# First branch's merge products issued directly behind the gate projections, in the attention's PSUM banks and in buffers of the normed input

## The chip, the core and the metric

One core of a Trainium2 chip runs the whole kernel as one program. The metric is the device time of one execution in microseconds (us), as a median over runs. Engines by their names in the profile: PE is the TensorE matmul unit, PEld its weight loads, DVE the VectorE, ACT the ScalarE, POOL the GpSimd, SP the SyncE, which issues most DMAs. Each engine works through its own instructions strictly in the order of its list, and waits for the other engines by semaphores.

## The reference

One layer over 1024 tokens of width 1024. Cut to what matters here:

```python
h = rmsnorm(x, g_pre_mix)
proj = h @ w_in                 # S5 input, conv inputs, q, k, v, forget logits, 3 x 1024 gate logits
y_a = s5_mixer(...)             # (1024 tokens, 512)
y_b = short_conv_mixer(...)     # (1024, 512)
y_c = forgetting_attention(...) # (1024, 512), 8 heads x 64, causal
gates = sigmoid(gate_logits + b_gate)          # three gates of 1024 channels
merged = (gates[0] * (y_a @ wa) + gates[1] * (y_b @ wb) + gates[2] * (y_c @ wc))
mix = merged @ w_out
x = x + rmsnorm(mix, g_post_mix)
x = x + rmsnorm(squared_relu(rmsnorm(x, g_pre_mlp) @ w_ff1) @ w_ff2, g_post_mlp)
```

The three branches a, b, c are numbered 0, 1, 2 in the kernel. The three products with `wa`, `wb`, `wc`, weighted by the gates and summed, are the "merge".

## The kernel before

**Number format.** Every matmul operand is kept as a pair of float32r tiles, a high part (H) and the rest (L), made by `split` (lines 72 to 77): ACT copies the operand into H, DVE subtracts H from the operand into L. `mm3` issues three matmuls per pair (H·H, H·L, L·H). A product over 512 input channels, 128 output channels and 512 tokens is thus 4 x 3 = 12 matmuls into one PSUM bank.

**Order of the work.** The input projections come first, fed by the generator `proj_stream` from the list `todo`; the attention follows, and takes the rest of the projections as filler between its own steps: the gate projections `g0` to `g22`, the last of them held back in `reserve`. Each gate tile goes through `proj` (tile `p_g`, tag `pj`, 2 PSUM banks), `gate_cons` applies a tanh on ACT into an SBUF tile of pool `gp` (tag `gt`, 2 buffers), and a DMA stores it to DRAM (`gt_s`). Within the attention, `scores` makes a score bank `ps` (tag `s`, 2 buffers), DVE takes its maximum, ACT the exponential into `P`, DVE scales it; `trans` transposes `P` on PE (`pt`) and splits it into `PT`; `av_` multiplies with V (`av`) and ACT (`lo`) and DVE (`yc`) take the result out. Head group 3's `yc` is stored to DRAM last (line 1061).

**After the attention** the pools of the attention are closed. Branch outputs of the first token half (`th` = 0) were stored to DRAM and are read back by `y_load` (tile `yr`, 1 MB in four DMAs, into the tag `raw` of pool `ws`, 2 buffers, shared with every raw weight tile), and split by `y_split` into `yH` and `yL` in pool `ext` (tag `e8`, 6 buffers). Branch 0's output lies time-major, so its four pieces are read with strides. Then 24 merge products per token half follow: `merge_item(th, dp, b)` does two of them, for the output tiles 2·dp and 2·dp + 1 of branch b, in the order b = 0, 1, 2 for each dp. Each needs its weight (`r_wb` loaded, split to `wb_0H` and `wb_0L`, 3 buffers each), its y pair, and a gate tile read back from DRAM (`gl`, 4 buffers). The product stands in a PSUM tile `pb` of pool `mp` (tag `m`, 8 banks). For b = 0 DVE writes gate x product to the accumulator `ma` (pool `mg`); for b = 1, 2 DVE writes it in place of the gate and POOL adds it to `ma`. After b = 2, `ma` is split into the tiles `m` (pool `big`, tag `t8`, 8 buffers: the same ones that held the normed input `hT`). `run_items` loads weights up to two items ahead and splits one item ahead. The second half's `yr` tiles, the four output projections `wo` and so on follow.

**What decides where an instruction stands.** The program is written in the order above, but except inside the blocks marked `manual_schedule` the engines' lists are made by a scheduler at build time, which may pull later work up into earlier work. A buffer of a rotating tag is handed on when its last reader is done; the waiting is done by the first writer of the new tile, in its engine's queue.

## Time and profile before

| what | value |
|---|---|
| median of 3 runs | 1704.85 us (1703.64 to 1709.92) |
| profiled execution, its own time | 1708.72 us |
| its span, first to last instruction | 1707.0 us |
| PE busy | 1622.3 us, 95% of the span |
| DVE, ACT, POOL busy | 1029.8, 693.2, 499.0 us |
| DMA moved | 261.73 MB, 153 GB/s over the span |
| mean granted TensorE clock | 0.980 |

The page of the profile gives busy times and groups; the timeline lists instructions in time with, in square brackets, how long the engine sat idle before one and who ended that; the view of waits sums these; the windows view gives, per stretch, each engine's busy time with its instruction count, the granted clock, the DMA share and GB/s. Names are tile names without their numbers, output on the left of the arrow. SPq and ACTq rows are DMA issues. A matmul's row shows its latency; successive rows overlap, so the pace is read from the differences of starts.

### The profile page before, as it was taken

To read this page: it belongs to the slowest core of one execution; us is meant where nothing else is said; L and a number is where in the kernel's file an instruction comes from. 1 tells how busy PE (TensorE), PEld (TensorE's weight loads), DVE (VectorE), ACT (ScalarE), POOL (GpSimd) and SP (SyncE) were. 2 spreads that over 40 slices of the span, in tenths; PEclk is the share of its full clock that TensorE was granted. 3 is DMA by queue.
4 is the path that set the end of the run, shared out by engine and by line. 5 is a ranking of instruction groups with operands and counts; after the bars stand their busy time and mean duration, and the time that the engine had idled before them with its cause. 6 is when DMAs were issued, how large, how long until landed. Compare 5 with 4: busy or idle time off the path is not lost.

```text
span 1707.0 us, 21044 instructions
## 1 busy us (share of the span) xinstructions
PE 1622.3 (95%) x7815; PEld 1335.7 (78%) x7815; DVE 1029.8 (60%) x1548; ACT 693.2 (41%) x1042; POOL 499.0 (29%) x603
## 2 busy tenths in 40 slices
PE   7999999999999999997899989699999999999998
PEld 6778778879888787876677768578778878888886
DVE  4768655433264564655564674778888765545565
ACT  4312112231354554555343234554454454443442
POOL 1085643100422303120232552344434300101143
PEclk9999999999999999999899989899999999999999
DMA  5412322330744526331872562356654499755521
GB/s 161 121 41 77 83 86 82 112 93 10 239 152 167 185 75 228 100 142 39 266 250 93 184 223 87 105 161 192 197 189 142 156 334 383 259 198 187 184 99 50
DMA packets 186034, 261.73 MB, mean 153 GB/s; under 512 B 24752, under 2 KB 108764, under 8 KB 183884
## 3 DMA queue, kind: packets, MB, share of 16 engines
q1 hardware_dynamic: 170380, 228.93, 41.9%
q10 hardware_dynamic: 15552, 31.46, 4.9%
q8 instruction: 61, 1.00, 0.2%
q14 instruction: 41, 0.34, 0.1%
HBM read 183.54 MB, written 75.63 MB: 152 GB/s over the span
## 4 chain that ended last, share of the span: by engine, by line
PE 68%; DVE 8%; DMA 4%; POOL 4%; ACT 3%; issue 3%; SPq 1%; DVEq 0%; ACTq 0%; POOLq 0%
PE p_g L122 14%; PE P L122 12%; PE p_q L122 4%; PE pb L122 3%; PE pv L122 3%; PE P4f L122 3%; PE P7f L122 3%; PE P6f L122 3%; PE P5f L122 3%; PE P2f L122 3%; PE P3f L122 3%; PE P1f L122 2%; PE ps L122 2%; PE av L122 2%; PE pt L126 2%
## 5 line engine op out<-in xcount | busy, mean ns | idle before, releaser
L65 DVE TENSOR_TENSOR st<-x,st 128x1024 fp32r<-128x1024 f32 x70 | 86.7, 1251 | 77.5 <-ACT st L73 74.5
L122 PE MATMUL p_g<-hT,w_g_1H 128*128 128x512 f32 x384 | 126.8, 408 | 4.7 <-ACT g L831 3.5
L122 PE MATMUL p_g<-hT,w_g_0H 128*128 128x512 f32 x384 | 126.5, 406 | 2.8 <-DVE ac L65 2.8
L73 ACT ACTIVATE st<-x 128x1024 fp32r<-128x1024 f32 x70 | 73.6, 1059 | 98.5 <-PE P6f L122 16.6
L65 POOL TENSOR_TENSOR w2s<-w2s 128x512 f32<-128x512 f32 x32 | 43.4, 1356 | 228.5 <-DMA w2s<-in_w_ff 219.3
L65 POOL TENSOR_TENSOR s<-w1r 128x512 f32<-128x512 f32 x32 | 52.8, 1671 | 167.0 <-DMA w1r<-in_w_ff 153.7
L65 POOL TENSOR_TENSOR ma<-ma,gl 128x512 f32<-128x512 f32 x32 | 50.0, 1573 | 145.8 <-DVE gl L68 145.8
L122 PE MATMUL pb<-yH,wb_0H 128*128 128x512 f32 x192 | 78.0, 406 | 12.5 <-ACT wb_0H L73 12.5
L122 PE MATMUL pb<-yH,wb_0L 128*128 128x512 f32 x192 | 77.7, 405 | 12.3 <-DVE wb_0L L65 12.3
L65 DVE TENSOR_TENSOR sl<-x,sh 128x1024 fp32r<-128x1024 f32 x42 | 56.6, 1352 | 47.4 <-ACT sh L73 47.4
L122 PEld LDWEIGHTS p_g<-hT,w_g_1H 128*128 128x128 f32 x384 | 69.3, 192 | 17.0 <-ACT g L831 3.9
L122 PEld LDWEIGHTS p_g<-hT,w_g_0H 128*128 128x128 f32 x384 | 70.2, 191 | 15.1 <-DVE ac L65 3.2
L65 POOL TENSOR_TENSOR fa<-fa,gfin 128x512 f32<-128x512 f32 x16 | 25.5, 1606 | 178.0 <-ACT fjk L1644 178.0
L122 PE MATMUL pb<-yL,wb_0H 128*128 128x512 f32 x192 | 77.0, 401 | 0.0
L122 PE MATMUL p_g<-hT,w_g_0L 128*128 128x512 f32 x192 | 76.8, 400 | 0.0
L122 PE MATMUL p_g<-hT,w_g_1L 128*128 128x512 f32 x192 | 76.3, 397 | 0.0
L65 DVE TENSOR_TENSOR PT<-pt,PT 128x512 fp32r<-128x512 f32 (+2 forms) x96 | 53.1, 553 | 32.1 <-ACT PT L73 31.5
L73 ACT ACTIVATE PT<-pt 128x512 fp32r<-128x512 f32 (+2 forms) x96 | 46.9, 489 | 48.5 <-PE pt L126 47.0
L73 ACT ACTIVATE sh<-x 128x1024 fp32r<-128x1024 f32 x42 | 44.2, 1058 | 51.4 <-PE P3f L122 9.9
L1023 ACT ACTIVATE P<-ps,mx 128x128 f32<-128x128 f32 (+3 forms) x64 | 47.3, 740 | 33.1 <-DVE mx L1020 30.7
L1020 DVE TENSOR_REDUCE mx<-ps 128x1 f32<-128x128 f32 (+3 forms) x64 | 48.0, 751 | 13.3 <-PE ps L122 13.1
L122 PEld LDWEIGHTS pb<-yH,wb_0L 128*128 128x128 f32 x192 | 37.5, 195 | 23.2 <-DVE wb_0L L65 15.2
(827 smaller groups left out, 4601.3 us busy)
## 6 DMA issues: line engine op xcount, KB each, us to landing
w2s<-in_w_ff SPq DMA_DIRECT2D x16, 1024.0 KB, 5.0
w1r<-in_w_ff SPq DMA_DIRECT2D x16, 1024.0 KB, 8.6
as<-sa SPq DMA_DIRECT2D x16, 1024.0 KB, 6.7
x<-as SPq DMA_DIRECT2D x32, 512.0 KB, 10.8
x<-t_P SPq DMA_DIRECT2D x32, 512.0 KB, 5.2
r_g<-in_w_in SPq DMA_DIRECT2D x12, 1024.0 KB, 5.8
gt_s<-g ACTq DMA_DIRECT2D x48, 256.0 KB, 2.0
t_P<-w2s SPq DMA_DIRECT2D x48, 256.0 KB, 2.7
```

The lines of the kernel that those rows point to most:

```text
L65: (eng or dve).tensor_tensor(o, x, y, op=op)
L73: act.activation(hi, src, AF.Copy, scale=scale)
L122: pe.matmul(o, l, r, start=start, stop=stop)
L126: pe.transpose(o, i, idn)
L1020: dve.tensor_reduce(mx, sv, axis=mybir.AxisListType.XY, op=MAX, negate=True)
L1023: act.activation(Pm[:, 0:kend].rearrange("p (c n) -> p c n", c=nch), sv, AF.Exp, bias=mx, accum_out=sm)
```

## The change

The four items of branch 0 in the first token half (eight products) are taken out of the merge loop and issued directly behind the last gate projection, before the attention's pools are closed. To that end

- their PSUM tiles come from the tag `pj` (2 banks, those of the projections) in place of the 8 banks of `m`,
- their gate tiles come from the tag `gt` of `gp` (2 buffers) in place of the 4 of `gl`,
- their accumulators are slices of two tiles in the tag `t8`, so that branches 1 and 2 add onto those,
- `yH` and `yL` of branch 0 go to the tag `t8` as well, into buffers of the first token half of `hT`, which the last gate projections read,
- branch 2's raw output goes to the tag `e8` of `ext` in place of `raw`,
- the tiles `m` are taken at the first item of branch 1,
- the first weights, branch 0's raw output and its split are asked for at counted steps of the gate projections.

```diff
@@ y_load
         if th:
             raw = big.tile([P, 4, HALF], F, name=f"yr{th}{b}", tag="t8", bufs=8)
+        elif b == 2:
+            raw = ext.tile([P, 4, HALF], F, name=f"yr{th}{b}", tag="e8", bufs=6)
         else:
             raw = ws.tile([P, 4, HALF], F, name=f"yr{th}{b}", tag="raw", bufs=2)
@@ y_split
-        yh = ext8(f"yH{th}{b}", [P, 4, HALF])
-        yl = ext8(f"yL{th}{b}", [P, 4, HALF])
+        yh, yl = [(ext8 if th or b else big8)(f"y{n}{th}{b}", [P, 4, HALF]) for n in "HL"]
@@ merge_item
-            if dp == 0 and b == 0:
+            if dp == 0 and b == (0 if th else 1):
                 for kh in range(2):
                     for hl in range(2):
                         mT[hl, th, kh] = big8(f"m{hl}{th}{kh}", [P, 4, HALF])
+            early = th == 0 and b == 0
             if b == 0:
                 for d in range(2):
-                    macc[d] = mg.tile([P, HALF], F, name=f"ma{th}{dp}{d}", tag="ma", bufs=4)
+                    macc[d] = maccs[dp // 2][:, dp % 2 * 2 + d] if early else \
+                        mg.tile([P, HALF], F, name=f"ma{th}{dp}{d}", tag="ma", bufs=4)
+            elif th == 0:
+                for d in range(2):
+                    macc[d] = maccs[dp // 2][:, dp % 2 * 2 + d]
...
-                gt = mg.tile([P, HALF], F, name=f"gl{th}{dt_}{b}", tag="gl", bufs=4)
+                if early:
+                    gt = gp.tile([P, HALF], F, name=f"gl{th}{dt_}{b}", tag="gt", bufs=2)
+                    ps = pp.tile([P, HALF], F, name=f"pb{th}{dt_}{b}", tag="pj", bufs=2)
+                else:
+                    gt = mg.tile([P, HALF], F, name=f"gl{th}{dt_}{b}", tag="gl", bufs=4)
+                    ps = mps(f"pb{th}{dt_}{b}")
                 sp.dma_start(gt, gt_s[b * 8 + dt_][:, sl])
-                ps = mps(f"pb{th}{dt_}{b}")
@@ the main sequence
-    mg0 = [merge_item(0, dp, b) for dp in range(4) for b in range(3)]
+    mga = [merge_item(0, dp, 0) for dp in range(4)]
+    mg0 = [merge_item(0, dp, b) for dp in range(4) for b in (1, 2)]
...
-    for _ in range(4):
-        next(ps_)
-    for b in range(3):
-        raw = y_load(0, b)
-        for _ in range(6):
-            next(ps_)
-        yT[0, b] = y_split(0, b, raw)
-        if b == 1:
-            mg0[0].split()
-            mg0[1].split()
-    while next(ps_) is not DONE:
-        pass
+    left = 16 * len(todo) + 64
+    raw = None
+    while True:
+        more = next(ps_) is not DONE
+        if raw is None and not todo:
+            raw = y_load(0, 0)
+            left = 32
+        left -= 1
+        if left == 14:
+            mga[0].split()
+        if left == 6:
+            maccs = [big.tile([P, 4, HALF], F, name="macc0", tag="t8", bufs=8)]
+            yT[0, 0] = y_split(0, 0, raw)
+            maccs.append(big.tile([P, 4, HALF], F, name="macc1", tag="t8", bufs=8))
+        if not more:
+            break
+    assert (0, 0) in yT
+    run_items(mga[:1], mga[1:])
+    run_items(mga[1:2], mga[2:])
+    raw1 = y_load(0, 1)
+    run_items(mga[2:3], mga[3:])
+    yT[0, 1] = y_split(0, 1, raw1)
+    raw2 = y_load(0, 2)
+    run_items(mga[3:], mg0)
+    yT[0, 2] = y_split(0, 2, raw2)
     es1.close()
...
-    run_items(mg0[:6], mg0[6:])
+    run_items(mg0[:4], mg0[4:])
     yraw = [y_load(1, b) for b in range(3)]
-    run_items(mg0[6:], wo0)
+    run_items(mg0[4:], wo0)
```

**Where the scheduler puts it.** First PE, at the end of the attention, before: `p_g_11` is the last gate projection, `pt` and `av` the last transposes and value products (four transposes of one tile are one row).

```order
L126 MATMUL pt_7015<-ident,P_6967 128x128 x4
L122 MATMUL p_g_11_7208<-hT_179,w_g_1H 128x512
L122 MATMUL p_g_11_7208<-hT_178,w_g_1L 128x512
L126 MATMUL pt_7022<-ident,P_6967 128x128 x3
L126 MATMUL pt_7028<-ident,P_7008 128x128 x4
L126 MATMUL pt_7035<-ident,P_7008 128x128 x4
L122 MATMUL av_7042<-PT_73_7014,V_3151 128x256
```

The last three groups of transposes stand one behind the other here, and the first merge product comes only after all 16 matmuls of `av_7042`. PE in the changed kernel, at the end of the gate projections:

```order
L122 MATMUL p_g_11_7174<-hT_178,w_g_1H 128x512
L126 MATMUL pt_6972<-ident,P_6941 128x128 x4
L122 MATMUL p_g_11_7174<-hT_179,w_g_1H 128x512
L122 MATMUL p_g_11_7174<-hT_178,w_g_1L 128x512
L122 MATMUL pb_7223<-yH_7182,wb_0H 128x512
L122 MATMUL pb_7223<-yL_7183,wb_0H 128x512
L122 MATMUL pb_7223<-yH_7182,wb_0L 128x512
```

The gate projections end two groups of transposes earlier, and the merge products `pb` take their place. Still PE in the changed kernel, some 35 rows on:

```order
L122 MATMUL pb_7239<-yH_7182,wb_0H 128x512
L122 MATMUL pb_7239<-yL_7183,wb_0H 128x512
L122 MATMUL pb_7239<-yH_7182,wb_0L 128x512
L122 MATMUL pb_7261<-yH_7182,wb_0H 128x512
L126 MATMUL pt_7028<-ident,P_7008 128x128 x4
L122 MATMUL pb_7261<-yL_7183,wb_0H 128x512
```

Between the last four groups of transposes now stand 9, 6 and 10 matmuls of merge products; in all, 38 of the 96 are issued before the attention's last value product, and 58 behind it. From the first `wo` product on, the order on PE is the one of before.

ACT, in the third query block of the last head, before: `PT` is the copy of transposed probabilities, `P` the exponential, `lo` the copy out of `av`.

```order
L73 ACTIVATE PT_63_6777<-pt_6803 128x4x128
L73 ACTIVATE PT_63_6777<-pt_6810 128x4x128
L1023 ACTIVATE P_6860,sm_6861<-ps_6854,mx_6858 128x384
L1056 ACTIVATE lo_6834<-av_6817 64x256
L73 ACTIVATE PT_70_6848<-pt_6850 128x128
```

The same place in the changed kernel:

```order
L73 ACTIVATE PT_63_6777<-pt_6803 128x4x128
L73 ACTIVATE yH_7182<-yr_7079 128x512 x4
L73 ACTIVATE PT_63_6777<-pt_6810 128x4x128
L1023 ACTIVATE P_6860,sm_6861<-ps_6854,mx_6858 128x384
L1056 ACTIVATE lo_6834<-av_6817 64x256
```

The four pieces of branch 0's `yH`, which stood behind the whole attention, are now in the middle of it, ahead of an exponential; on DVE the four pieces of `yL` stand correspondingly. `yH` waits there for the last gate projection of the first token half to let go of its buffer of `hT`.

SP, the queue of loads, behind the last store of weight sums (`t_P`), before: `r_wb` are branch weights, `gl` gates read back.

```order
L1112 DMA t_P_170<-w2s_6703 128x512
L1231 DMA gl_7255<-gt_s_107 128x512
L1231 DMA gl_7271<-gt_s_108 128x512
L1231 DMA gl_7293<-gt_s_115 128x512
L1231 DMA gl_7310<-gt_s_116 128x512
L1188 DMA r_wb_7159<-in_w_branch 128x4x256
```

And in the changed kernel, where another `r_wb` already stands ahead of this place:

```order
L1112 DMA t_P_170<-w2s_6703 128x512
L1189 DMA r_wb_7214<-in_w_branch 128x4x256
L1189 DMA r_wb_7216<-in_w_branch 128x4x256
L1189 DMA r_wb_7254<-in_w_branch 128x4x256
L1242 DMA gl_7222<-gt_s_107 128x512
L1141 DMA yr_7292<-yb_s_99 128x512
L1141 DMA yr_7292<-yb_s_100 128x512
L1242 DMA gl_7238<-gt_s_108 128x512
```

All four weights of branch 0 are asked for ahead of the gates; the first of them stands before the last load of weight sums. In this list the second gate tile comes behind two pieces of branch 1's output (`yr` from `yb_s`), whose buffer comes free when the third weight is split.

## Prediction

> **What bounds the kernel now.** PE is busy for 95% of the span, so the question is where it is not. I read the waits between 780 and 1000 us first, PE's and then SP's (who waited for whom: us in total, times, longest).
>
> ```profile
> PE pb L122 <- ACT wb_0H L73: 12.5, 2, 12.3
> SPq L1231 <- DMA yc_s<-yc: 58.5, 1, 58.5
> SPq L1188 <- DVE yL L65: 5.5, 3, 2.4
> ```
>
> PE sits idle once for 12.3 us ahead of the first merge product. The timeline of PE around it (start, us, what, idle before) and the windows (stretch, its length, then busy us of PE, PEld, DVE, ACT, POOL, then clock, DMA share, GB/s):
>
> ```profile
> 796.17 0.40 PE L122 MATMUL p_g<-hT,w_g_1L 128*128 128x512 f32 x1
> 797.51 0.55 PE L126 MATMUL pt<-ident,P 128*128 128x128 f32 x3 [0.95 <-DVE PT L65]
> 799.23 0.66 PE L126 MATMUL pt<-ident,P 128*128 128x128 f32 x4 [1.17 <-DVE PT L65]
> 801.30 1.12 PE L126 MATMUL pt<-ident,P 128*128 128x128 f32 x4 [1.41 <-DVE PT L65]
> 802.07 3.00 PE L122 MATMUL av<-PT,V 128*128 128x256 f32 x16
> 817.39 0.79 PE L122 MATMUL pb<-yH,wb_0H 128*128 128x512 f32 x1 [12.32 <-ACT wb_0H L73]
> 821.26 0.39 PE L122 MATMUL pb<-yH,wb_0L 128*128 128x512 f32 x1
> 841.25 0.39 PE L122 MATMUL pb<-yH,wb_0H 128*128 128x512 f32 x1
> ...
> 796.50:817.40 20.90, 5.05 (x29) 4.37 (x28) 9.29 (x12) 9.69 (x12) 0.00 (x0) 0.68 0.45 154
> 817.40:821.30 3.90, 3.86 (x9) 2.61 (x10) 2.36 (x2) 1.06 (x1) 0.00 (x0) 0.52 0.84 291
> ```
>
> Once the gate projections run out at 796.5, PE has only 11 transposes and 16 value products left, each waiting for a split, and then nothing. The cause is an order of release, not a shortage of any engine: the queue of loads stands on buffers of the attention until its last store is done, then on the splits of branch 0 and 1's outputs, and only then asks for the first branch weight.
>
> ```profile
> 807.49 3.90 DVE L65 TENSOR_TENSOR yL<-yr,yH 128x512 fp32r<-128x512 f32 x4 [1.56 <-ACT yH L73]
> 808.62 1.80 SPq L1231 DMA_DIRECT2D gl<-gt_s  x4
> 811.42 0.38 SPq L1188 DMA_DIRECT2D r_wb<-in_w_branch  x1
> 816.28 1.06 ACT L73 ACTIVATE wb_0H<-r_wb 128x1024 fp32r<-128x1024 f32 x1 [4.18 <-DMA r_wb<-in_w_branch]
> ```
>
> The weight is issued at 811.42, lands at 816.28, and PE starts 1.1 us later. From 821.26 to 841.25 run 88 matmuls, 0.227 us each; a merge product of 12 is 2.73 us.
>
> **The change part by part.** *What it removes.* From 796.5 to 817.4 PE's real work is 11 transposes and 16 value products. At the full-clock pace of rows such as these (four transposes from 776.41 to 776.76, eight value products and one gate matmul's start at 777.79)
>
> ```profile
> 776.41 0.60 PE L126 MATMUL pt<-ident,P 128*128 128x128 f32 x4
> 776.76 1.19 PE L122 MATMUL av<-PT,V 128*128 128x256 f32 x8
> 777.79 0.39 PE L122 MATMUL p_g<-hT,w_g_1H 128*128 128x512 f32 x1
> ```
>
> that is 11 x 0.09 + 16 x 0.13, about 3.1 us; of 20.9 us, 17.8 are lost. Then the first eight matmuls take 821.26 - 817.39 = 3.87 us where 8 x 0.227 = 1.82 would do, at a granted clock of 0.52: 2.05 more. The Trainium skill ("TensorE: Matmul & The Clock Gate", Part 1) says that an idle window of some 3.4 us halves the clock until PE has been busy for as long; an estimate from that is 1.7 us in place of 2.05, and the trace agrees within the 0.35. The eight products of branch 0 are 8 x 2.73 = 21.8 us of work with everything at hand, more than the 19.85 us that are lost, and they now stand between the last transposes and behind the last value product. The hole is thus covered if their inputs are early. They are: their weights now stand ahead of the gates in SP's list, and `yr` of branch 0 is loaded where it was before.
>
> *What it costs in the attention.* The four strided pieces of `yH` on ACT and of `yL` on DVE move from behind the attention into it.
>
> ```profile
> 774.62 0.60 ACT L73 ACTIVATE PT<-pt 128x512 fp32r<-128x512 f32 x1 [1.02 <-PE pt L126]
> 777.04 0.60 ACT L73 ACTIVATE PT<-pt 128x512 fp32r<-128x512 f32 x1 [1.82 <-PE pt L126]
> 777.54 0.57 ACT L1023 ACTIVATE P<-ps,mx 128x384 f32<-128x384 f32 x1
> 778.00 0.20 ACT L1023 ACTIVATION_READ_ACCUMULATOR P<-ps,mx 128x1 f32 x1
> 778.26 0.42 PE L122 MATMUL ps<-K,Q 128*128 128x320 f32 x1
> 879.38 4.22 ACT L73 ACTIVATE yH<-yr 128x512 fp32r<-128x512 f32 x4
> ```
>
> Four such pieces take 4.22 us on ACT. They go into the 1.82 us of idle time before the second of these `PT` copies, so this copy and the exponential behind it come 4.22 - 1.82 = 2.4 us late. The exponential is what frees one of the two score banks: it ended at 778.20, and PE began the next scores at 778.26. There is no slack, so PE stalls 2.4 us. Behind it DVE's `yL` ends about one piece (1.06 us) after `yH`, and the copies catch up, since ACT is busy 9.78 of the 16 us up to 796.
>
> ```profile
> 780.00:796.00 16.00, 16.00 (x98) 12.91 (x97) 12.02 (x25) 9.78 (x22) 0.00 (x0) 1.00 0.05 17
> ```
>
> DVE with 12.02 of 16 catches up more slowly; the splits of the second to fourth weight (1.06 on ACT, 1.23 on DVE each) also stand there. I take 2.4 + 0.5 = 2.9 us; bounds 0 (if slack elsewhere in the queue absorbs it) and 4.2 + 1.2 = 5.4 (nothing absorbed, one weight split besides).
>
> *What holds the eight products.* With 2 PSUM banks product k + 2 waits until DVE has read product k. That read is one operation of 0.69 us, and it needs the gate tile, loaded after the read two products earlier.
>
> ```profile
> 822.38 0.69 DVE L68 SCALAR_TENSOR_TENSOR ma<-gl,pb 128x512 f32<-128x512 f32 x1 [1.03 <-PE pb L122]
> gl<-gt_s SPq DMA_DIRECT2D x28, 256.0 KB, 6.0
> r_wb<-in_w_branch SPq DMA_DIRECT2D x12, 512.0 KB, 4.8
> yr<-yc_s SPq DMA_DIRECT2D x8, 256.0 KB, 7.4
> ```
>
> (Size, and median us from issue to landing, between 780 and 900.) Issue 0.4, landing, read 0.69: with 6.0 us a round takes 7.1, while two products take 5.45. But the first four products are stretched over some 16 us by the rest of the attention, so their gates have time. For the last four the gates of products 7 and 8 stand behind the weight of branch 2 and the four pieces of branch 2's output. SP asks for these when the first weight of branch 1 is split; that split needs the buffer of the second weight, free when product 4 ends. Counted in 2.73 us products from the gates' end at about 797, with 3.1 us of attention between them, product 4 ends at 797 + 10.9 + 3.1, and 2.9 us late from the stall is already in the 797: about 811 to 813. Two splits on ACT and DVE (2.3 us), five issues (2 us) and 6 us later, at 822 to 823.5, gate 7 is there, and gate 8 about 1.5 us behind, once `yL` of branch 1 (2.3 us) is through DVE: 825. PE would have finished product 8 at 797 + 21.8 + 3.1 + 2 = 824, the 2 us for the gaps between late transposes. The next product, in a bank that replaces the two, waits for that last read: 825 + 0.7 against 824, so 1.5 us lost (bounds 0 and 4.5, the latter with gates landing in 9 us).
>
> *What comes later.* The other 16 products are 43.6 us; their weights and gates, the second half's `yr` and the first `wo` weight have to come in that time. Before, the second-half loads held up one weight and one gate:
>
> ```profile
> 844.54 4.32 SPq L1136 DMA_DIRECT2D yr<-ya_s  x3
> 854.55 0.38 SPq L1188 DMA_DIRECT2D r_wb<-in_w_branch  x1
> 855.19 7.61 DMA gl<-gt_s
> 863.34 0.50 PE L122 MATMUL pb<-yH,wb_0H 128*128 128x512 f32 x1 [0.17 <-ACT wb_0H L73]
> 864.76 0.50 PE L122 MATMUL pb<-yH,wb_0L 128*128 128x512 f32 x1 [0.69 <-DVE wb_0L L65]
> 886.20 0.39 PE L122 MATMUL wo000p<-wo_0H,m 128*128 128x512 f32 x1
> ```
>
> PE lost only 0.86 us then. The weight that follows these loads in the new order is that of branch 1 for the last `dp`, needed 12 products in, at 825.7 + 32.7 = 858.4. The loads begin about 840 (behind a gate tile that comes free with POOL's add for the fourth of these products, which PE ends at 825.7 + 10.9), take some 10 us of issue as before (844.54 to 854.55), the weight lands 6 us later, and DVE's split waits behind a gate that needs 7.6: about 861. So 2.1 us in place of 0.86, 1.2 us more (bounds 0 and 6). None of the three losses can come out below nothing, since no work is taken away at these places.
>
> *Sum.* 17.8 + 2.05 - 2.9 - 1.5 - 1.2 = 14.2 us gained when `wo000p` starts: 872 in place of 886.20. From there PE's list is as before, and what it waits for (POOL's and DVE's norm steps, weights) is started by PE's own progress, so the lead stays. Against the profiled execution, 1708.72, that makes 1694.5; that execution lies 3.9 us above the median, 1704.85, so the forecast is 1704.85 - 14.2 = 1690.6, say 1691. With no losses the sum is 19.85 (1685); with all the upper bounds, 19.85 - 5.4 - 4.5 - 6 = 4 us (1701).
>
> **The rivals.** *A: the merge becomes a matter of loads.* What must still land after 815.5 is about 14.7 MB (7 branch weights, 16 + 2 gates, 4 MB of `yr`, two gain rows, one `wo` weight).
>
> ```profile
> 815.00:870.00 55.00, 51.71 (x217) 41.59 (x218) 28.14 (x32) 16.01 (x16) 13.99 (x10) 0.94 0.87 273
> 870.00:890.00 20.00, 19.84 (x88) 16.11 (x87) 16.69 (x17) 10.99 (x11) 6.65 (x4) 1.00 0.63 209
> ```
>
> At 273 GB/s this is 53.8 us, done at 869, just in time for 872; the point from which loads decide is 260 GB/s. At the middle of these two rates, 241, it takes 61 us, and with the last weight's splits `wo000p` starts at 879: 7 us gained, 1698. For it: the DMA share is 0.87 already. Against: the stretch from 817.4 to 821.3, quoted first, moved 291 GB/s at a share of 0.84, so there is some room.
>
> *B, slower: the ring of two banks and two gates.* Each read of a product stands on DVE ahead of the splits for the next transposes, so a late gate stops the attention as well. The Trainium skill ("Perfetto Trace Analysis", Matmul Optimizations) advises using all eight PSUM banks, which speaks against moving these products to two; no run here shows yet what it costs. The 0.69 us read alone, against a product of 2.73, would cost PE nothing. As a mechanism of this kernel: three rounds depend on a landing L, each losing L + 1.1 - 5.45 us. At 6.0 us that is 1.65 a round; the 14.2 us and the 1.5 already counted are used up at L = 9.6, and with L = 13, 26 us are lost and the kernel stands at 1715. Against it: between 796.5 and 817.4 the DMA share is only 0.45, and 7.61 is the longest stretch on a gate in the chain above.
>
> *C: the lead is given back.* Between 980 and 1000 PE loses 7.2 us to norm steps and splits.
>
> ```profile
> 980.00:1000.00 20.00, 12.79 (x48) 10.03 (x48) 13.40 (x14) 7.83 (x12) 10.15 (x20) 0.74 0.53 172
> ```
>
> If these were held by something that does not move with PE, by DMA traffic for instance, the lead would vanish in such stretches: 1704, no change. Against it: the share there is 0.53.
>
> **How the numbers follow.** Forecast 0.76, A 0.15, C 0.05, B 0.04. A difference of 0.5% (8.5 us) is about what a measurement of this kernel can tell. Nearly all of the forecast's case (0.73) is faster than that, 0.03 not; of A, 0.05 is faster and 0.10 within; C is within; B slower, and 0.01 of the case within that turns out worse is counted as slower as well: 0.78, 0.17, 0.05. The range reaches from 1686, where hardly any of the three losses comes, to 1700, which takes in A's middle and most of the upper bounds.
>
> **What would show it.** Right: no idle stretch over 3 us of PE between 796 and 825, a granted clock of 1.0 there, `wo000p` near 872, one stall of some 2 us at scores behind the strided `yH`, a short wait at the first product of branch 1. Wrong: PE waiting for score banks or `PT` several times between 776 and 800 (the attention's price was too low); many `pb` waits for `ma` reads with DVE waiting for `gl` (B); waits on `wb_0H` behind DMA after 825 at a share near 1 (A); `wo000p` early but the end not (C).

## The result and the profile after

| | before | changed |
|---|---|---|
| median, 7 runs each on one chip | 1709.92 us (1703.64 to 1712.24) | 1695.55 us (1692.83 to 1699.76) |
| ratio, 95% interval | | 0.9923, 0.9909 to 0.9936: about 13.1 us faster |
| profiled execution, its own time / span | 1708.72 / 1707.0 | 1695.55 / 1693.8 |
| PE busy | 1622.3 us, 95% | 1622.6 us, 96% |
| mean granted TensorE clock | 0.980 | 0.983 |

PE does the same work in a shorter span. The idle times of PE between 765 and 875 us in the changed kernel (start, us, what, idle before and who ended it), and the first output projection:

```profile
785.31 0.86 PE L122 MATMUL ps<-K,Q 128*128 128x320 f32 x4 [1.83 <-ACT P L1023]
811.72 0.66 PE L126 MATMUL pt<-ident,P 128*128 128x128 f32 x4 [0.34 <-DVE PT L65]
830.31 0.47 PE L122 MATMUL pb<-yH,wb_0H 128*128 128x512 f32 x1 [2.14 <-DVE macc L68]
874.37 0.39 PE L122 MATMUL wo000p<-wo_0H,m 128*128 128x512 f32 x1
```

The 12.32 us in front of the first merge product and the gaps of 0.95 to 1.41 us ahead of the last transposes are gone. Three waits of a new kind stand in their place: 1.83, 0.34 and 2.14 us. The two waits of 0.17 and 0.69 us for a weight at 863 us are gone as well. The windows over the same stretch (length, busy us of PE, PEld, DVE, ACT, POOL, then clock, DMA share, GB/s):

```profile
796.00:824.00 28.00, 27.66 (x149) 22.52 (x149) 17.16 (x26) 11.71 (x18) 0.00 (x0) 1.00 0.51 167
824.00:872.00 48.00, 45.75 (x201) 37.24 (x200) 31.29 (x34) 18.96 (x20) 20.01 (x13) 1.00 0.88 289
```

Where PE was busy for 5.05 of 20.9 us at a clock of 0.68, it is now busy for 27.66 of 28 at 1.00. The merge moves 289 GB/s.

How much the stretch itself gained is read from a common point. Up to the gate copy at 686 us both programs issue the same list (before first, then changed):

```profile
686.44 0.69 ACT L831 ACTIVATE g<-p_g,bgcol 128x512 f32<-128x512 f32 x1
```

```profile
688.33 0.69 ACT L831 ACTIVATE g<-p_g,bgcol 128x512 f32<-128x512 f32 x1
```

The changed kernel's execution is 1.9 us late there by chance. From this copy to the first output projection `wo000p` it takes 874.37 - 688.33 = 186.04 us, against 886.20 - 686.44 = 199.76 before: 13.7 us less. From `wo000p` to the end of the span it is 819.4 against 820.8, so the lead is kept. I call the distance from this copy to `wo000p` "the stretch" below. It comes from one execution of each kernel: in the table below its gains lie up to 3.3 us off those of the times, most of them below, and in the last row 4.7, so the one of before may be a short one.

The new waits, seen from the engines that were waited for. ACT, then SP, then DVE:

```profile
780.04 4.17 ACT L73 ACTIVATE yH<-yr 128x512 fp32r<-128x512 f32 x4
784.59 0.58 ACT L1023 ACTIVATE P<-ps,mx 128x384 f32<-128x384 f32 x1
```

```profile
819.45 0.38 SPq L1189 DMA_DIRECT2D r_wb<-in_w_branch  x1
819.88 1.97 SPq L1141 DMA_DIRECT2D yr<-yc_s  x4
821.90 1.98 SPq L1242 DMA_DIRECT2D gl<-gt_s  x2
```

```profile
809.24 0.69 DVE L68 SCALAR_TENSOR_TENSOR macc<-gl,pb 128x512 f32<-128x512 f32 x1 [0.87 <-DMA gl<-gt_s]
826.15 1.23 DVE L65 TENSOR_TENSOR wb_0L<-r_wb,wb_0H 128x1024 fp32r<-128x1024 f32 x1 [2.62 <-ACT wb_0H L73]
828.77 1.40 DVE L68 SCALAR_TENSOR_TENSOR macc<-gl,pb 128x512 f32<-128x512 f32 x2 [1.39 <-DMA gl<-gt_s]
```

At 780 the four strided pieces of `yH` stand ahead of a copy and of the exponential that ends at 785.2; PE's scores start at 785.31. At 819 to 824 SP asks for a weight, four pieces of branch 2's output and only then for the gates of products 7 and 8. DVE, strictly in its order, first waits 2.62 us for ACT's part of a weight's split and then 1.39 us for the gates, and reads products 7 and 8 at 828.77; PE goes on at 830.31. The wait of 0.34 us has the same kind of cause: ahead of 809.24 DVE waits 0.87 us for a gate, and so it comes late to the transposes that PE waits for at 811.72.

### The profile page after: what moved, and what is told of

Same layout as the page of the kernel before. It is cut to its first block, busy times and chain, and to the rows that moved or that the text cites. A ratio compares the mean times of both kernels' runs of the same rounds, so it can differ in the third digit from the quotient of the medians.

```text
span 1693.8 us, 21052 instructions
## 1 busy us (share of the span) xinstructions
PE 1622.6 (96%) x7815; PEld 1334.8 (79%) x7815; DVE 1032.2 (61%) x1548; ACT 693.6 (41%) x1042; POOL 501.9 (30%) x603
## 4 chain that ended last, share of the span: by engine, by line
PE 64%; DVE 9%; POOL 5%; DMA 5%; issue 4%; ACT 3%; SPq 1%; DVEq 0%; ACTq 0%; POOLq 0%
PE p_g L122 13%; PE P L122 11%; PE pb L122 3%; PE p_q L122 3%; PE pv L122 3%; PE P4f L122 3%; PE P7f L122 3%; PE P3f L122 3%; PE P6f L122 3%; PE P5f L122 3%; PE P2f L122 3%; PE P1f L122 2%; PE ps L122 2%; PE av L122 2%; PE pt L126 2%
## 5 line engine op out<-in xcount | busy, mean ns | idle before, releaser
L65 POOL TENSOR_TENSOR macc<-macc,gl 128x512 f32<-128x512 f32 x16 | 27.8, 1748 | 101.6 <-DVE gl L68 101.6
L1020 DVE TENSOR_REDUCE mx<-ps 128x1 f32<-128x128 f32 (+3 forms) x64 | 48.1, 752 | 13.2 <-PE ps L122 13.1
```

Source lines behind the costliest of these rows:

```text
L65: (eng or dve).tensor_tensor(o, x, y, op=op)
L1020: dve.tensor_reduce(mx, sv, axis=mybir.AxisListType.XY, op=MAX, negate=True)
```

## The experiments

All stand against the kernel of before on the same chip.

| kernel | median, us | ratio, 95% interval | the stretch, us |
|---|---|---|---|
| before | 1707.57 to 1709.92 | 1 | 199.76 |
| the change | 1695.55 | 0.9923, 0.9909 to 0.9936 | 186.04 |
| products behind the attention | 1699.67 | 0.9951, 0.9933 to 0.9970 | 193.79 |
| same, tail filled with useless matmuls | 1700.76 | 0.9952, 0.9934 to 0.9971 | 194.46 |
| y buffers undone | 1706.59 | 0.9990, 0.9977 to 1.0002 | 200.95 |
| y buffers undone, products behind | 1701.67 | 0.9954, 0.9936 to 0.9973 | 195.16 |
| gates ahead of branch 2's output | 1691.29 | 0.9905, 0.9886 to 0.9923 | 183.37 |
| that output loaded twice | 1699.10 | 0.9942, 0.9920 to 0.9965 | 192.08 |
| split on GpSimd | 1694.09 | 0.9920, 0.9902 to 0.9938 | 188.13 |
| both (gates ahead, split on GpSimd) | 1691.59 | 0.9895, 0.9877 to 0.9913 | 183.61 |
| both, with two copies on GpSimd | 1691.92 | 0.9896, 0.9868 to 0.9923 | 184.93 |
| before, hole filled with 235 small matmuls | 1707.96 | 0.9997, 0.9983 to 1.0011 | 203.92 |

**Products behind the attention.** The inputs stay early, the eight products go back:

```diff
-                if early:
-                    gt = gp.tile([P, HALF], F, name=f"gl{th}{dt_}{b}", tag="gt", bufs=2)
-                    ps = pp.tile([P, HALF], F, name=f"pb{th}{dt_}{b}", tag="pj", bufs=2)
...
+                gt = mg.tile([P, HALF], F, name=f"gl{th}{dt_}{b}", tag="gl", bufs=4)
+                ps = mps(f"pb{th}{dt_}{b}")
...
     assert (0, 0) in yT
+    mga[1].split()
+    es1.close()
...
     run_items(mga[:1], mga[1:])
...
-    es1.close()
```

> The inputs stay as early as in the changed kernel (first weights, branch 0's output and its split in the attention, accumulators), but the eight products stand behind the whole attention again, in 8 banks and with 4 gate buffers. Theory E (the hole was a matter of late inputs; where the products stand adds only the gaps of the tail): PE idles 0.95 + 1.17 + 1.41 = 3.5 us between the last transposes and about 1 us until the old banks are let go, but the first product follows the last value product directly, the clock stays at 1.0, and the 2.14 us wait for a read on two banks goes: some 2.4 us slower than the changed kernel, so about 10.7 us faster than before. Theory F (the products' work as filler carries the gain): most of the 12.3 us hole returns and with it the slow clock, less than 5 us faster than before. The stall of 1.8 us behind the strided yH stays in both.

Measured: 8.4 us faster than before (5.1 to 11.4), the stretch 7.8 us longer than in the changed kernel. PE in the tail, and two windows there (the clock stands before the last two numbers):

```profile
798.41 0.40 PE L122 MATMUL p_g<-hT,w_g_1L 128*128 128x512 f32 x1
800.02 0.44 PE L126 MATMUL pt<-ident,P 128*128 128x128 f32 x2 [1.22 <-DVE PT L65]
802.14 0.68 PE L122 MATMUL av<-PT,V 128*128 128x256 f32 x4 [0.73 <-DVE PT L65]
804.69 0.55 PE L126 MATMUL pt<-ident,P 128*128 128x128 f32 x3 [1.41 <-DVE PT L65]
806.40 0.92 PE L126 MATMUL pt<-ident,P 128*128 128x128 f32 x4 [1.17 <-DVE PT L65]
808.74 1.11 PE L126 MATMUL pt<-ident,P 128*128 128x128 f32 x4 [1.41 <-DVE PT L65]
809.51 3.73 PE L122 MATMUL av<-PT,V 128*128 128x256 f32 x16
813.03 0.66 PE L122 MATMUL pb<-yH,wb_0H 128*128 128x512 f32 x1
```

```profile
798.00:806.00 8.00, 3.88 (x27) 2.76 (x24) 4.39 (x8) 4.35 (x9) 0.00 (x0) 1.00 0.47 152
808.00:810.00 2.00, 1.26 (x6) 1.26 (x7) 0.69 (x1) 0.11 (x1) 0.00 (x0) 0.50 0.00 0
```

The first product does follow the last value product with no wait, and there is no wait on banks, as theory E says. But the tail's gaps are 5.9 us, not 3.5, and the clock falls to 0.50 with no gap over 1.41 us: the last 16 value products take 813.03 - 809.51 = 3.5 us, where eight took 1.03 at full clock (777.79 - 776.76, in the prediction). So by the times early inputs alone bring more than half of the gain, as E has it, and the products as filler the rest, which F saw; by the stretch it is 6.0 us of 13.7, a little less than half. Late in the stretch PE also waited 0.98 and 0.78 us for a weight here, and not 2.14 for the banks.

**The same with a filled tail.** 28 matmuls of the products' size, whose result nobody reads, go behind the gate projections of the kernel with the products behind the attention:

```diff
+    warm = pp.tile([P, HALF], F, name="warm", tag="pj", bufs=2)
+    for i in range(28):
+        mm(warm, mga[0].w[0][0][:, i % 4, 0:P], yT[0, 0][0][:, i % 4, :], i == 0, i == 28 - 1, 0.214)
     es1.close()
```

> The kernel with early inputs and the eight products behind the attention, and 28 more matmuls of the products' size whose result nobody reads, 6, 4, 7, 6 and 5 of them between the last groups of transposes; the rest of the computation is the same. Without them PE had gaps of 0.73 to 1.41 us there, none longer, and ran at a granted clock of 0.50 to 0.66 from 806 to 813. Theory K (a sparse PE is enough to halve the clock, and that is part of what the merge products bring as filler): the clock stays at 1.0, the last value product's 16 matmuls take 2.1 us in place of 3.5, the late transposes lose 0.3 to 0.5 us each, and though PE does 6.4 us of useless work it finishes the attention 1.5 to 2.5 us earlier: faster than without the filler by about 2 us. Rival L (the clock had another cause, the gaps are too short to matter): the clock falls as before, and the time is the same or some 0.5 to 1 us longer, since 6 to 7 matmuls are more than a gap of 1.4 us takes.

PE at the scores and in the tail, and one window of each:

```profile
785.63 0.86 PE L122 MATMUL ps<-K,Q 128*128 128x320 f32 x4 [1.82 <-ACT P L1023]
801.50 0.39 PE L122 MATMUL p_g<-hT,w_g_1L 128*128 128x512 f32 x1
814.64 0.45 PE L122 MATMUL pb<-yH,wb_0H 128*128 128x512 f32 x1
```

```profile
804.00:816.00 12.00, 11.28 (x68) 9.15 (x67) 4.65 (x8) 3.04 (x6) 0.00 (x0) 1.00 0.29 100
788.00:790.00 2.00, 2.00 (x7) 1.61 (x7) 1.00 (x4) 1.62 (x5) 0.00 (x0) 0.50 0.19 68
```

The clock holds at 1.00 through the tail, and from the last gate matmul to the first product it takes 814.64 - 801.50 = 13.1 us in place of 813.03 - 798.41 = 14.6, with 6.4 us of useless work inside. That is theory K's mechanism, at its lower end. In the time it doesn't show: the ratio is the same within its interval, as rival L had it, though L had the clock fall. In the profiled execution the clock halved at another place, at 788, behind the stall of 1.82 us at the scores; behind the same stall it had held at 1.00 in the changed kernel.

**The y buffers undone.**

```diff
-        yh, yl = [(ext8 if th or b else big8)(f"y{n}{th}{b}", [P, 4, HALF]) for n in "HL"]
+        yh, yl = [ext8(f"y{n}{th}{b}", [P, 4, HALF]) for n in "HL"]
```

> One line of the change undone: branch 0's yH and yL go back into the buffers of pool ext, free only when the attention is over; the weights stay early. Theory E: the splits then run where they ran before, from about 806 to 811, so PE idles some 4 to 6 us behind the last value product in place of 12.3, with the tail's 3.5 us and a part of the slow clock; the 1.8 us stall in the attention goes. 6 to 9 us faster than before. A rival (only the late weight made the hole): the first product starts within 1 us of the last value product, and the gain is that of the changed kernel, 13 us, or more, since the stall is saved.

Measured 1.7 us faster than before, an interval that includes none, so my 6 to 9 us were wrong and the rival's 13 more so. PE in this kernel:

```profile
810.33 0.50 PE L122 MATMUL pb<-yH,wb_0H 128*128 128x512 f32 x1 [2.38 <-ACT yH L73]
811.47 0.80 PE L122 MATMUL pb<-yL,wb_0H 128*128 128x512 f32 x1 [0.64 <-DVE yL L65]
825.14 0.50 PE L122 MATMUL pb<-yH,wb_0H 128*128 128x512 f32 x1 [1.10 <-DVE macc L68]
839.16 0.76 PE L122 MATMUL pb<-yH,wb_0H 128*128 128x512 f32 x1 [2.85 <-DVE macc L68]
```

The hole is even shorter than expected (3.0 us). But PE, starting late, runs into the ring of two banks twice, for 3.95 us, and the tail and its slow clock stand unfilled. DVE waited for no gate there: the first of these reads stands at 824.40 behind branch 1's `yL`, which itself starts late, at 822.19, and the second at 838.34 behind branch 2's. To take the ring out, the products then went behind the attention in 8 banks and with 4 gate buffers as well (the two diffs above together):

> The kernel with only the y buffers undone gained some 1 us, where 6 to 9 were expected. Here the same, but the eight products stand behind the attention in 8 banks with 4 gate buffers, so that the waits for reads on two banks (1.10 and 2.85 us there) can't occur. Theory S (there the tail's gaps, 5.3 us, a hole of 3.0, half a clock over some 12 us and the two bank waits together ate what the earlier weights gave): the hole of about 3 us and the slow clock stay, the bank waits go, about 4 us faster than that kernel, 5 us faster than before. Rival T (the waits are for gates that come late whatever the banks): the same waits stand at the eight banks or a little later, and the time is as with two.

```profile
812.96 0.50 PE L122 MATMUL pb<-yH,wb_0H 128*128 128x512 f32 x1 [2.39 <-ACT yH L73]
```

7.9 us faster than before, 6 us faster than with two banks; the hole is the same to 0.01 us and no wait for a bank is left. Theory S, with a larger price than the 3.95 us that PE was seen to wait: 5.8 us of the stretch. Rival T is out: the read behind branch 1's `yL` comes late here too, at 828.88, and PE doesn't wait. The two kernels also say that y in the `hT` buffers brings nothing by itself that shows (0.9954 against 0.9951, each within some 3 us): it only pays where the products come forward.

**Gates ahead of branch 2's output.**

```diff
-    raw2 = y_load(0, 2)
     run_items(mga[3:], mg0)
+    raw2 = y_load(0, 2)
```

> Branch 2's raw output is asked for behind the gates of products 7 and 8 and not ahead of them. Theory G (the 2.14 us wait of the first branch 1 product comes from those gates, which queue behind four pieces and a weight): the wait falls to under 0.5 us, 1.5 to 2 us faster than the changed kernel, unless branch 2's split becomes late in turn (it has some 5 us of product time to spare). Rival (the wait comes from the two banks and the read itself, or from the weight's split on VectorE ahead of the read): the wait stays at about 2 us.

PE, then DVE, in this kernel:

```profile
825.42 0.47 PE L122 MATMUL pb<-yH,wb_0H 128*128 128x512 f32 x1 [0.87 <-DVE macc L68]
859.54 0.50 PE L122 MATMUL pb<-yH,wb_0L 128*128 128x512 f32 x1 [0.74 <-DVE wb_0L L65]
```

```profile
822.38 1.23 DVE L65 TENSOR_TENSOR wb_0L<-r_wb,wb_0H 128x1024 fp32r<-128x1024 f32 x1 [2.46 <-ACT wb_0H L73]
824.59 0.69 DVE L68 SCALAR_TENSOR_TENSOR macc<-gl,pb 128x512 f32<-128x512 f32 x1 [0.38 <-PE pb L122]
```

The wait falls by 1.27 us, about the 1.39 that DVE had waited for the gates. The remaining 0.87 is the read of product 8 itself: DVE is through with the weight's split at 823.6 and with product 7 at 824.2, idles 0.38 us until PE ends product 8, and reads it in 0.69. So both my theory and the first half of its rival hold, the two banks and the read; the weight's split holds nothing up. The time is 16.2 us below before, 3 us better than the change, though the two intervals overlap. Now that PE is earlier, the weight at 859.54 is late.

**That output loaded twice.** The opposite dose:

```diff
                 sp.dma_start(raw[:, ct, :], src[ct][:, sl])
+                if th == 0 and b == 2:
+                    sp.dma_start(raw[:, ct, :], src[ct][:, sl])
```

> The changed kernel, but each of the four pieces of branch 2's raw output is loaded twice into the same place, ahead of the gates of products 7 and 8; the second four wait in the queue of loads until the first four have landed, some 6 us. Theory G (the wait at the first product of branch 1 is the lateness of these gates): the wait of 2.14 us grows by 6 to 8 us, to 8 or 10, and the time by as much, less than 1 us of it made up later. Theory R (two of rival B's kind: the ring has slack of its own): the wait grows by less than 3 us.

```profile
832.88 0.76 PE L122 MATMUL pb<-yH,wb_0H 128*128 128x512 f32 x1 [6.44 <-DVE macc L68]
```

```profile
824.00:872.00 48.00, 41.56 (x174) 33.93 (x173) 28.41 (x30) 15.08 (x15) 18.94 (x11) 0.93 0.88 277
```

In time this kernel is 9.9 us faster than before, 3.2 less than the change, with intervals that overlap. The wait grows by 4.3 us to 6.44, less than the 6 to 8 that I expected but beyond the rival's 3. The stretch grows by 6.0: behind so long a wait the clock falls too, to 0.93 in the mean of 48 us, where it was 1.00. Late gates do stop PE at the two banks.

**The split on GpSimd.** Branch 0's eight operations in `y_split` for the first half:

```diff
-                split(yh[:, ct, :].rearrange("p (c t) -> p c t", t=T),
-                      yl[:, ct, :].rearrange("p (c t) -> p c t", t=T),
-                      raw[:, ct, :].rearrange("p (t c) -> p c t", t=T))
+                sh, sl_, sr = (yh[:, ct, :].rearrange("p (c t) -> p c t", t=T),
+                               yl[:, ct, :].rearrange("p (c t) -> p c t", t=T),
+                               raw[:, ct, :].rearrange("p (t c) -> p c t", t=T))
+                if th:
+                    split(sh, sl_, sr)
+                else:
+                    ts(sh, sr, 1.0, MUL, eng=pool)
+                    tt(sl_, sr, sh.bitcast(F), SUB, pool)
```

> Branch 0's strided split goes to GpSimd, copy and difference, eight operations in the place of four on ScalarE and four on VectorE. GpSimd is idle there. Theory H (the 1.83 us stall at the scores comes from the 4.17 us of yH ahead of the exponential that frees a score bank): the stall goes, y is ready about 15 us later but the first product at 800 has that slack; 1.8 us faster than the changed kernel. Rivals: GpSimd is too slow with strides (over 15 us for the eight) and the first product waits, slower than the changed kernel; or the stall stays, because something else holds the bank.

PE, then DVE, in this kernel:

```profile
829.21 0.47 PE L122 MATMUL pb<-yH,wb_0H 128*128 128x512 f32 x1 [3.45 <-DVE macc L68]
```

```profile
786.90 0.54 DVE L65 TENSOR_TENSOR PT<-pt,PT 128x384 fp32r<-128x384 f32 x1
787.36 1.39 DVE L60 TENSOR_SCALAR P<-P,sm 128x640 f32<-128x640 f32 x1
825.57 2.29 DVE L65 TENSOR_TENSOR yL<-yr,yH 128x2048 fp32r<-128x2048 f32 x1 [4.68 <-ACT yH L73]
827.78 1.28 DVE L68 SCALAR_TENSOR_TENSOR macc<-gl,pb 128x512 f32<-128x512 f32 x2
```

The stall at the scores is gone, as theory H has it, and the time is that of the changed kernel: the scheduler now puts branch 2's `yL` ahead of the reads of products 7 and 8 in DVE's list, `yL` waits for its data, and the first product of branch 1 waits 3.45 us. Three small waits of 0.26 to 0.45 us for VectorE's part of transposes are new too.

**Both, and a milder form of it.**

> Both earlier edits at once: branch 0's split on GpSimd, and branch 2's raw output asked for behind two more gates. Alone, the first took the 1.83 us stall away and gave it back as a wait of 3.45 us for a read on two banks, because VectorE's list then had branch 2's split, with its late data, ahead of the reads of products 7 and 8; the second cut that wait to 0.87. Here the reads stand ahead of that split. Theory M (each wait is set by what stands ahead in one engine's list, so the two gains add): no stall, a wait of 1 us or less, 1.5 to 2 us faster than with the second edit alone, about 18 us faster than before. Rival N (the gates come at a time that the end of the attention sets, so that PE, when it is earlier, only waits longer): the wait grows by what the stall gave back, about 16 us faster than before, as with the second edit alone.

PE, then DVE:

```profile
824.68 0.47 PE L122 MATMUL pb<-yH,wb_0H 128*128 128x512 f32 x1 [0.87 <-DVE macc L68]
```

```profile
823.84 0.69 DVE L68 SCALAR_TENSOR_TENSOR macc<-gl,pb 128x512 f32<-128x512 f32 x1 [2.00 <-PE pb L122]
```

17.9 us faster than before (14.9 to 21.0); the wait stayed at 0.87, as theory M has it and N doesn't. DVE was idle for 2.00 us ahead of the last read, so no split had a part in that wait. M's gain of 1.5 to 2 us over the gates alone isn't shown: the ratios, 0.9895 and 0.9905, differ by less than their intervals, and the stretch is no shorter: four small waits of 0.27 to 0.43 us have come for the stall. In the milder form only the pieces 2 and 3 are copied on GpSimd, and all differences are made on DVE:

```diff
-                if th:
+                if th or ct < 2:
                     split(sh, sl_, sr)
                 else:
                     ts(sh, sr, 1.0, MUL, eng=pool)
-                    tt(sl_, sr, sh.bitcast(F), SUB, pool)
+                    tt(sl_, sr, sh.bitcast(F), SUB)
```

> As the kernel with both edits, but GpSimd copies only two of the four strided pieces; ScalarE copies the other two and VectorE makes all four differences. ScalarE's two pieces take 2.1 us against 1.3 to 1.8 us that it idles there; GpSimd is busy for 4 us in place of 14. Theory P (with all eight operations on GpSimd, VectorE's scalings of P, from SBUF to SBUF, took 0.85 and 1.39 us in place of 0.49 and 0.56, and that is what made the small waits of 0.29 to 0.43 us for transposes): the stall of 1.8 us falls to under 0.6, the small waits all but go, PE loses less than 1.5 us in all between 775 and 830, 0.5 to 1 us faster than with everything on GpSimd, about 18 us faster than before. Rival: the two pieces on ScalarE alone still stall PE by 1 us or more, and nothing is gained.

```profile
778.14 0.87 PE L122 MATMUL ps<-K,Q 128*128 128x320 f32 x4 [0.31 <-ACT P L1023]
780.49 1.43 PE L122 MATMUL av<-PT,V 128*128 128x256 f32 x8 [1.48 <-DVE PT L65]
```

The stall at the scores falls to 0.31 us; but now the differences, three in a row on DVE, hold a `PT` for 1.48. The time is the same, 17.8 us below before. Each place of these strided pieces costs PE some 1 to 2 us; I found none that is free. By their ratios these two kernels are the fastest tried, but against the change their intervals overlap.

**The slow clock by itself.** In the kernel of before, small matmuls behind the last value product, 180 and then 235:

```diff
+    warm = mps("warm")
+    for i in range(180):
+        mm(warm[:, 0:P], identb, maskb, i == 0, i == 180 - 1, 0.05)
     run_items(mg0[:6], mg0[6:])
```

> The kernel of before, with 180 small matmuls (128x128, bf16, result unread) put behind the last value product, some 9 to 10 us of the hole of 12.3. They change no input and no order of the loads. Theory K: the first eight matmuls of the merge run at full clock, 1.8 us in place of 3.87, and nothing else moves: some 2 us at the start of the first output projection, less than a timing can tell. Rival: these matmuls are too small to count as work, and the clock is at 0.5 as before.

```profile
822.23 0.80 PE L122 MATMUL pb<-yH,wb_0H 128*128 128x512 f32 x1 [3.51 <-ACT wb_0H L73]
```

The 180 took 10.2 us and left a gap of 3.51 us, because the weight came later than in before; behind it the first eight matmuls took 3.99 us, against 3.87 before. That kernel has one execution, 1714.58 us. With 235:

> The same as the kernel with 180 small matmuls in the hole of before, now 235. The 180 took 10.2 us at a granted clock of 1.0 and left a gap of 3.51 us, behind which the merge's first matmuls ran at 0.50 again; 55 more fill another 3.1 us. Theory K: with less than a microsecond left of the gap the clock stays at 1.0 and the first eight matmuls of the merge take 1.8 to 2 us in place of 3.87; the first output projection starts some 2 us earlier than in before, counted from the same gate of the attention, which a timing hardly tells. Rival: the clock falls at the change of operands or of form, whatever the gap, and the eight take 3.4 us or more again.

```profile
822.70 0.50 PE L122 MATMUL pb<-yH,wb_0H 128*128 128x512 f32 x1 [2.23 <-ACT wb_0H L73]
823.96 0.50 PE L122 MATMUL pb<-yH,wb_0L 128*128 128x512 f32 x1 [0.53 <-DVE wb_0L L65]
```

```profile
823.00:824.00 1.00, 0.47 (x3) 0.04 (x1) 0.91 (x1) 0.00 (x0) 0.00 (x0) 1.00 0.56 218
825.00:826.00 1.00, 1.00 (x4) 0.74 (x3) 0.59 (x1) 0.38 (x1) 0.00 (x0) 0.50 0.78 231
```

Again the weight came later, and the gap was 2.2 us and not under 1, with another of 0.53 two matmuls on. The small matmuls had run at a clock of 1.00 (810 to 820), and it still stood at 1.00 from 823 to 824, with the new operands; from 825 on it was 0.50. So the clock didn't fall at the change of operands; it fell later, and the first eight matmuls took 3.65 us. But whether it would have held behind a gap of less than 1 us this run doesn't tell, and the 2.05 us could not be had apart from the rest: that term stays unproven by itself. The ratio is 1 within 0.2%, as both theories allow.

## Why the prediction was right, point by point

The forecast was 14.2 us, measured are 13.1 (10.9 to 15.6) in the time and 13.7 in the stretch. The absolute 1691 was for a median of before of 1704.85 from three runs; seven runs gave 1709.92, and the change stands at 1695.55. `wo000p` was to start at 872 and started at 874.37, of which 1.9 us are the execution's late start.

- **What is removed, 19.85 us: right in place and cause, some 0.5 us too large, and it needs both halves of the change.** The gaps and the slow clock are gone; the size is taken up below. The experiments divide it: early weights and inputs alone bring some 8 us (0.9951 and 0.9954), the products as filler in the tail the remaining 5; by the stretch it is 6 and 8. The reason that I gave first, an order of release, covers only the first part.
- **The attention, 2.9 us: 1.83 measured.** The place, the cause and the queue were right: four pieces, 4.17 us, ahead of the exponential that frees a score bank. For the 0.5 us of consequences no wait is seen. The wait of 0.34 us at 811.72 isn't one of them: it comes from a late gate (809.24), as rival B has it, and where DVE doesn't wait for that gate, in the kernel with the gates ahead, it is missing.
- **The two banks, 1.5 us: 2.14 measured, and 0.34 with them.** Gates 7 and 8 were late behind the weight and four pieces, as worked out: 1.27 us go with early gates. The other 0.87 is the last read, which the forecast had in its sum as 0.7 (825 + 0.7 against 824 is 1.7, where 1.5 was taken). Left out was the late gate before them, at 809.24.
- **The late weight, 1.2 us more: failed, no wait to speak of came.** In the changed kernel, DVE:

```profile
862.52 1.22 DVE L65 TENSOR_TENSOR wb_0L<-r_wb,wb_0H 128x1024 fp32r<-128x1024 f32 x1
```

  The loads began at 841.62, where I had some 840, and the weight's second part was ready at 863.7, where I had 861. But PE came to this weight not at 858.4 but at 830.31 + 32.7 = 863.0, and so the 0.86 us of before went too, though the forecast held that this loss could not come out below nothing. My end of the eight products, 825.7, was 4.6 us too early, 1.9 of them the late start. Where PE is earlier, in the kernel with the gates ahead, the wait is there: 0.74 us at 859.54. The term was real and had the same slack as the one before it: the two can't be added.
- **The rivals.** A: PE waits for no weight between 824 and 872, at 289 GB/s, above the 260 at which loads were to decide. B: the mechanism is real. The Trainium skill's rule to use all eight banks ("Perfetto Trace Analysis", Matmul Optimizations) shows its price where gates or y are late: 6.44 us of waiting with late gates, and some 6 us between the two kernels with undone y, which are 0.9990 and 0.9954 and differ in gate buffers too, 2 against 4. In the change as it stands it costs 2.14 us, and 0.34 by the late gate. C: the lead at `wo000p` is the lead at the end.

That the sum came within 1.1 us owes something to luck: the attention's loss was 1.1 us smaller and the late weight's was not there, while the banks and gates took 1.0 more and what is removed was too large. By the measured terms the stretch should have gained 19.85 + 0.86 - 1.83 - 0.34 - 2.14 = 16.4 us, and it gained 13.7. Of the 2.7 between, 1.2 are two idle times of PE ahead of 765 us, 0.61 and 0.55, that the execution of before didn't have. One like the second, for an exponential at 754, stands in nine of the ten kernels built on the change and in none of the three with the old order, so it seems to belong to the change; waits like the first come in both kinds. Where the other 1.5 went, two windows from the gate copy to `wo000p` show, before and changed:

```profile
686.44:886.20 199.76, 182.66 (x936) 148.09 (x935) 120.23 (x198) 95.42 (x167) 34.28 (x25) 0.96 0.48 156
688.33:874.37 186.04, 179.96 (x936) 144.99 (x935) 125.39 (x200) 95.16 (x167) 38.26 (x26) 1.00 0.50 163
```

With 936 instructions in each, PE's idle time fell from 17.1 to 6.1 us, nearly what the waits above come to. Its busy time fell by 2.7 us only, where the forecast's pace has 5.05 - 3.1 = 1.95 in the tail and 2.05 in the first eight matmuls, 4.0 together. That is 1.3 of the 1.5. Some 0.5 us of it lie in the tail: at 0.09 us a transpose and 0.13 a value product the forecast left out what PE takes at a change between kinds of matmuls. Behind the four transposes at 804.17 the next two products start at 804.55 and 804.87, 0.32 apart in place of 0.23, and in the changed kernel the tail with its 96 products took 27.5 us where that pace gives 27.0. So much of the 19.85 was work and not loss. Most of the other 0.8 lies ahead of 781 us: up to the transposes at 776.41 before and at 781.01 now PE was busy for 89.63 us with 498 instructions and for 91.02 with 501, and three gate matmuls are only 0.7. Why it took longer there stays open.

## What to carry to other kernels

Independent work moved into a tail of short dependent steps pays twice, since it also keeps the clock up; but first see whether the hole behind the tail is a late load, because that part can be had without moving the work. Ahead of adding up small losses along one chain, ask which of them use the same slack: a wait that makes PE later hides the next late load, and a stall that is removed may come back at the next item that isn't earlier. When a multi-piece step is moved, look at what stands behind it in the same engine's list, not at the engine's free time.

## What the runs showed of the hardware

- The granted clock fell to 0.50 with PE gaps of 0.73 to 1.41 us only, after PE had been busy for 3.88 of 8 us (products behind the attention, 798 to 806; 0.50 from 808 on). A lone stall of 1.8 us halved it in one execution (filled tail, at 788) and not in another (the changed kernel, at 785). The Trainium skill ("TensorE: Matmul & The Clock Gate", Part 1) gives an idle window of about 3.4 us; here no single gap had to be that long, which is nearer to what the same page tells of frequent micro-idles ("A second HAM failure mode: psum-queue depth-cycling").
- While POOL worked on the strided pieces, one of DVE's scalings of `P` from SBUF to SBUF took 1.39 us (640 columns, at 787.36 above), against this in the changed kernel:

```profile
791.09 0.56 DVE L60 TENSOR_SCALAR P<-P,sm 128x640 f32<-128x640 f32 x1
```

  The splits of 384 columns that read PSUM took the same time (0.54 at 786.90, against 0.56 at 792.12 in the changed kernel). The Trainium skill ("SBUF — State Buffer", SBUF: two separate sides) describes one pair of ports that these two engines take in turn, whole instructions at a time. That the scaling is slowed and the split from PSUM is not agrees with a shared pair; whole turns can't be read from it, since the scaling ended at 788.75, within two POOL copies that the profile has from 785.16 to 789.28.
